# Three seven-product pairs in eight instead of two, and two pairs whose low parts are summed by DMA

## The chip, the cores and the metric

The kernel runs on one core of a Trainium2 chip. The metric is device time in microseconds (us) of one execution. Three runs of the kernel before took 2014.81, 2015.30 and 2015.38 us (median 2015.3). Engines: PE (TensorE, matmuls), PEld (its weight loads), DVE (VectorE), ACT (ScalarE), POOL (GpSimd), SP (SyncE, which here only issues DMAs).

## The reference

A decoder trunk of two layers on 256 tokens of width 2048, in float32. Each layer has attention (layer 0 a sliding window, layer 1 a block form that for 256 tokens is plain causal attention), attention to 256 memory tokens, and a feed-forward part of width 8192:

```
D_MODEL, SEQ, DEPTH, D_FF = 2048, 256, 2, 8192
mix = concat([self_out, mem_out]) @ w_o[layer]
h = layer_norm(ALPHA * h + mix, ln_g[layer, 0], ln_b[layer, 0])
ffn = jnp.square(jax.nn.relu(h @ w_up[layer])) @ w_down[layer]
h = layer_norm(ALPHA * h + ffn, ln_g[layer, 1], ln_b[layer, 1])
```

The change touches only the line with `ffn`.

## The kernel before

Each float32 operand is split into a high part, rounded to the matmul's type (`hi`, cast by ACT, line 97), and a low part, the rest (`lo`, subtracted by DVE, line 98). A product of two operands takes three matmuls: high x high, high x low, low x high (`mm3`, lines 269 to 273). The stationary side is a 128x128 tile of activations, the moving side 512 columns of weights.

The feed-forward part runs in four chunks of 2048 hidden columns per layer. A chunk has two up groups (`v_` = 0 and 1, 1024 hidden columns each) and two down groups (1024 output columns each). A group, `mlp_group`, covers 256 tokens x 1024 columns x 2048 of depth as eight pairs of 128-deep tiles; each pair's weights are one tile `raw` of 1 MB, loaded by SP. Twenty-nine groups run this way, 15 up and 14 down; the other three take another form (`aform`).

A plain pair has eight products, 24 matmuls. A fast pair has seven products by Strassen's scheme, 21 matmuls: `fast_weights` forms four differences of the weights in a tile `t` (DVE, lines 117, 120, 121) and splits seven blocks; `fast_acts` forms four sums of the activations (`x_f`, then `sums`). Four of the products, P1, P5, P6 and P7, go to PSUM banks of their own, which take turns with the banks of the transposes `pt_h`; `early` combines them. `UP` and `DOWN` (lines 69, 70) give the order of the pairs and how many are fast: pairs 0 and 1 of (2, 3, 0, 4, 1, 5, 6, 7).

At an up group's end DVE adds the banks and ACT applies relu and square; the result `u_n` is transposed to `gT` by PE in the next group, at the places that `UHOOKS` (line 71) names as (position of the pair, bank). In the second up group of a chunk `fast_acts(gt)` forms the sums for the down groups (hooks (5, 0) and (6, 0)). The first up group of layer 0 forms its sums from `hT` by hooks (0, 0) and (1, 1).

All engines run their queues in order. The order in which the queues stand is set by a scheduler at build time, and so is which of a pool's buffers a tile gets. What a pair may run ahead is limited by the pools: four buffers shared by `raw`, `t` and `x_f` (`NRAW`), seven for `whi`, seven for `wlo` (`NHI`).

Of the kernel before, what the change touches and what calls it, by code (L numbers as in the profile page):

```python
# [8 lines left out]
F32 = mybir.dt.float32  # L9
F32R = mybir.dt.float32r  # L10
I32 = mybir.dt.int32
AF = mybir.ActivationFunctionType
ALU = mybir.AluOpType
AX = mybir.AxisListType

P = 128
# [17 lines left out]
NRAW = 4  # L34
# [31 lines left out]
NWARM = 2  # L66
FILL = (10, 11, 12, 16)

UP = ((2, 3, 0, 4, 1, 5, 6, 7), 2)
DOWN = ((2, 3, 0, 4, 1, 5, 6, 7), 2)  # L70
UHOOKS = ((0, 3), (1, 0), (1, 2), (1, 3))
WTAIL = ((1, 2), (2, 0), (3, 1), (5, 2), (7, 1), (9, 2))


# [1 line left out]
def trunk(ctx: ExitStack, tc: tile.TileContext, a: dict, out: bass.AP):  # L76
# [19 lines left out]
    def split(hi, lo, src):  # L96
        nc.scalar.copy(hi, src)  # L97
        nc.vector.tensor_tensor(lo, src, hi.bitcast(F32), ALU.subtract)  # L98
# [26 lines left out]
    def fast_acts(xs, units):  # L125

        parts = []
        for j in range(0, len(units), 2):  # L130
            n = len(units[j:j + 2])
            x = xs[j // 2][:, :2 * n]
            raw = wp.tile([P, 2, 8, P], F32, name="x_f", tag="raw", bufs=NRAW)
            f = raw[:, 0, :4 * n].rearrange("p (k t) c -> p k (t c)", t=2)
            nc.vector.tensor_tensor(f, x[:, :, 0].bitcast(F32), x[:, :, 1].bitcast(F32), ALU.add)
            a11, a21 = f[:, 0:2 * n:2, :P], f[:, 0:2 * n:2, P:]
            a12, a22 = f[:, 1:2 * n:2, :P], f[:, 1:2 * n:2, P:]
            s = raw[:, 1, :4 * n].rearrange("p (u q) c -> p u q c", q=4)
            nc.vector.scalar_tensor_tensor(s[:, :, 0], a21, -1.0, a22, op0=ALU.mult, op1=ALU.subtract)
            nc.vector.scalar_tensor_tensor(s[:, :, 1], s[:, :, 0], -1.0, a11, op0=ALU.mult, op1=ALU.subtract)  # L140
            nc.vector.tensor_tensor(s[:, :, 2], a11, a21, ALU.subtract)
            nc.vector.tensor_tensor(s[:, :, 3], a12, s[:, :, 1], ALU.subtract)
            parts += [s[:, u] for u in range(n)]
        yield
        for (hi, lo), s in zip(units, parts):
            split(hi, lo, s)
        yield

    def sum_units(n, tags):
        units = []  # L150
        for tag in tags[:n]:
            if tag == "pts":
                units.append([ap_.tile([P, 4, P], F32R, name="sums", tag="pts", bufs=2) for _ in range(2)])
            else:
# [100 lines left out]
    def mlp_group(src, xts, sums, hooks, early, order, nfast):  # L255

        ps = [ps_mm.tile([P, 512], F32, name="ps_g", tag="mm") for _ in range(4)]
        own = {}  # L260
        seen = {}
        last = {}

        fast = ("P1", 0, 1, "P5", "P7", "P6", 2)
        for u in order:
            for i in range(7 if u < nfast else 4):
                last[fast[i] if u < nfast else i] = (u, i)

        def mm3(bank, x, w, st, en):
            (xh, xl), (hi, lo) = x, w  # L270
            nc.tensor.matmul(bank, xh, hi, start=st, stop=False)  # L271
            nc.tensor.matmul(bank, xh, lo, start=False, stop=False)  # L272
            nc.tensor.matmul(bank, xl, hi, start=False, stop=en)  # L273

        def tok(k, t):
            return [xts[k // 4][:, k % 4, s, t * P:(t + 1) * P] for s in range(2)]

        left = nfast
        for pos, u in enumerate(order):
            k0, k1 = 2 * u, 2 * u + 1  # L280
            if u < nfast:
                for i in range(4):
                    hooks.get((pos, i), nothing)()
                if not own:
                    for nm in ("P1", "P5", "P6", "P7"):
                        own[nm] = ps_at.tile([P, 512], F32, name=nm, tag="at")
                w = fast_weights(src[u])
                sx = [[s[:, q] for s in sums[u]] for q in range(4)]
                prods = (("P1", tok(k0, 0), "B11"), (0, tok(k1, 0), "B21"), (1, sx[3], "B22"),
                         ("P5", sx[0], "T1"), ("P7", sx[2], "T3"), ("P6", sx[1], "T2"), (2, tok(k1, 1), "T4"))  # L290
                for i, (b, x, wn) in enumerate(prods):
                    mm3(own[b] if b in own else ps[b], x, w[wn], b not in seen, last[b] == (u, i))
                    seen[b] = True
                left -= 1
                if not left:
                    early(own)
                continue
            (h0, l0), (h1, l1) = weights(src[u])
            w = {"B11": (h0[:, :512], l0[:, :512]), "B22": (h0[:, 512:], l0[:, 512:]),
                 "B12": (h1[:, :512], l1[:, :512]), "B21": (h1[:, 512:], l1[:, 512:])}  # L300
            for b in range(4):
                hooks.get((pos, b), nothing)()
                t, n = b // 2, b % 2 + 1
                mm3(ps[b], tok(k0, t), w[f"B1{n}"], b not in seen, False)
                mm3(ps[b], tok(k1, t), w[f"B2{n}"], False, last[b] == (u, b))
                seen[b] = True
        return ps


# [287 lines left out]
    for l in range(LAYERS):  # L597
# [34 lines left out]
        for c in range(FF // CH):  # L632
            gt = new_acts("og", "gT")
            todo = []
            sum_g = sum_units(DOWN[1], ("v", "mk"))
            for v_ in range(CH // 1024):

                hooks = dict(zip(UHOOKS, todo))
                us = [None] * 4
                if c == 0 and v_ == 0 and not more:  # L640
                    for nb in range(2):
                        ps, fin = aform([a["wup_s"][nb, i] for i in range(4)], hT, hold=(16 if nb == 0 else 0))
                        if nb == 0:
                            us[0] = relu2(ps[0])
                            fin()
                            us[2] = relu2(ps[1])
                        else:
                            us[1], us[3] = relu2(ps[0]), relu2(ps[1])
                else:
                    if sum_h is None:  # L650
                        sum_h = sum_units(UP[1], ("sum_h0", "sum_h1", "pts"))
                        steps = fast_acts(hT, sum_h)
                        hooks[0, 0] = hooks[1, 1] = lambda s=steps: next(s)
                    if v_ == 1:
                        steps = fast_acts(gt, sum_g)
                        hooks[5, 0] = hooks[6, 0] = lambda s=steps: next(s)
                    acc = []
                    ps = mlp_group(a["wup"][l, c * (CH // 1024) + v_], hT, sum_h, hooks, sums_up(acc), *UP)
                    for b in range(4):
                        nc.vector.tensor_tensor(acc[b], acc[b], ps[b], ALU.add)  # L660
                        nc.scalar.activation(acc[b], acc[b], AF.Relu)
                        nc.scalar.activation(acc[b], acc[b], AF.Square)
                    us = acc

                def back(b, v_=v_, us=us, gt=gt):
                    transposed(us[b], gt[2 * v_ + b % 2], b // 2, 0)
                todo = [lambda b=b, f=back: f(b) for b in (0, 1, 2, 3)]
            last = c == FF // CH - 1
            if last and more:
                memt = load_acts(a["memt"], "hT", "memt")  # L670
            for v_ in range(D // 1024):
                if last and v_ == 1:
                    for nb in range(2, 4):
                        ps, fin = aform([a["wdn_s"][l, nb - 2, i] for i in range(4)], gt,
                                        hold=(0 if nb == 2 else 8 if more else HOLDF))
                        if nb == 2:
                            for t in range(NT):
                                residual(h, ps, t, nb, False, st)
                    continue
# [68 lines left out]
```

## Time and profile before

| | us |
|---|---|
| median of three runs | 2015.3 |
| the profiled execution's own time | 2016.56 |
| its span | 2014.4 |
| PE busy | 1994.2 (99%) |
| DVE busy | 1543.9 (77%) |
| ACT busy | 1046.0 (52%) |
| POOL busy | 1.2 |
| chain that ended last | PE 96%, DVE 3% |

What an engine is busy with is summed over the span; what bounds the kernel is read from the chain that ended last and from stretches. Instructions on one engine overlap a little: the duration of one is longer than the step from one start to the next, and it is the step that counts when many follow each other. PE's matmuls are pipelined in the same way.

### The profile page before, as it was taken

The page shows a single profiled execution, that of the slowest core. Times are in us where ns is not written, and L with a number is a line of the kernel's source. Part 1 is how long each engine was busy: PE and PEld are TensorE (multiplying, and loading weights), DVE is VectorE, ACT ScalarE, POOL GpSimd, SP SyncE. Part 2 cuts the span into 40 slices and gives each one's busy share as a digit, 9 for nine tenths or more (in the row PEclk, how much of TensorE's full clock was granted, in tenths as well). Part 3 has the DMA queues.
Part 4 walks back from the last instruction along what each step waited for, and adds up shares of the span by engine and source line. Part 5 has one row for each costly group of instructions (what it writes and reads, how often), then busy time and mean ns, then how long its engine had stood idle before and what let it go on. Part 6 is the DMA issues. An engine that isn't in the chain of part 4 may idle for free.

```text
span 2014.4 us, 23998 instructions
## 1 busy us (share of the span) xinstructions
PE 1994.2 (99%) x9326; PEld 1662.3 (83%) x9326; DVE 1543.9 (77%) x1961; ACT 1046.0 (52%) x1361; POOL 1.2 (0%) x8
## 2 busy tenths in 40 slices
PE   9999999999999999999999999999999999999997
PEld 7888888888888888888888888778888888888886
DVE  6566659988787888878785665688878887878885
ACT  6455534654564555466444554346455545654651
POOL 0000000000000000000000000000000000000000
PEclk9999999999999999999999999999999999999999
DMA  9644554555456555456654446445564555555651
GB/s 336 251 160 152 191 185 169 215 203 207 169 186 225 214 177 194 172 188 240 245 225 168 160 160 204 147 146 188 206 216 184 190 186 188 199 218 191 238 209 73
DMA packets 56273, 391.63 MB, mean 194 GB/s; under 512 B 6368, under 2 KB 6368, under 8 KB 9696
## 3 DMA queue, kind: packets, MB, share of 16 engines
q1 hardware_dynamic: 56160, 390.10, 53.7%
q8 instruction: 73, 1.20, 0.2%
q14 instruction: 40, 0.33, 0.0%
HBM read 387.98 MB, written 2.10 MB: 194 GB/s over the span
## 4 chain that ended last, share of the span: by engine, by line
PE 96%; DVE 3%; issue 0%; DMA 0%; ACT 0%; SPq 0%; DVEq 0%
PE ps_g L271 18%; PE ps_g L273 18%; PE ps_g L272 18%; PE ps_w L209 7%; PE ps_a L231 5%; PE ps_a L232 5%; PE ps_a L233 5%; PE ps_w L211 4%; PE P L271 3%; PE P L273 3%; PE P L272 3%; PE pt_h L443 2%; PE ps_m L553 1%; PE ps_m L554 1%; PE ps_m L555 1%; DVE h L436 1%
## 5 line engine op out<-in xcount | busy, mean ns | idle before, releaser
L98 DVE TENSOR_TENSOR wlo<-raw,whi 128x1024 fp32r<-128x1024 f32 (+1 forms) x706 | 818.1, 1174 | 329.7 <-ACT whi L97 325.2
L97 ACT CAST whi<-raw 128x1024 fp32r<-128x1024 f32 (+1 forms) x706 | 697.2, 1014 | 624.5 <-PE ps_g L273 349.7
L271 PE MATMUL ps_g<-whi,hT 128*128 128x512 f32 x780 | 306.7, 393 | 0.0
L273 PE MATMUL ps_g<-whi,hT 128*128 128x512 f32 x780 | 303.8, 390 | 0.0
L272 PE MATMUL ps_g<-wlo,hT 128*128 128x512 f32 x780 | 303.7, 389 | 0.0
L271 PE MATMUL ps_g<-whi,gT 128*128 128x512 f32 x728 | 286.4, 393 | 0.0
L273 PE MATMUL ps_g<-whi,gT 128*128 128x512 f32 x728 | 283.7, 390 | 0.0
L272 PE MATMUL ps_g<-wlo,gT 128*128 128x512 f32 x728 | 283.4, 389 | 0.0
L273 PEld LDWEIGHTS ps_g<-whi,hT 128*128 128x128 f32 x780 | 146.4, 188 | 30.8
L271 PEld LDWEIGHTS ps_g<-whi,hT 128*128 128x128 f32 x780 | 146.5, 188 | 29.4
L272 PEld LDWEIGHTS ps_g<-wlo,hT 128*128 128x128 f32 x780 | 146.6, 188 | 29.3
L273 PEld LDWEIGHTS ps_g<-whi,gT 128*128 128x128 f32 x728 | 136.7, 188 | 28.9
L97 ACT CAST whi<-t 128x1024 fp32r<-128x1024 f32 x116 | 122.0, 1052 | 72.5 <-PE ps_g L273 45.1
L272 PEld LDWEIGHTS ps_g<-wlo,gT 128*128 128x128 f32 x728 | 136.8, 188 | 27.3
L271 PEld LDWEIGHTS ps_g<-whi,gT 128*128 128x128 f32 x728 | 136.7, 188 | 27.2
L98 DVE TENSOR_TENSOR wlo<-t,whi 128x1024 fp32r<-128x1024 f32 x116 | 141.5, 1222 | 20.9 <-ACT whi L97 20.5
L209 PE MATMUL ps_w<-hT,whi 128*128 128x512 f32 x320 | 119.9, 414 | 0.0
L209 PE MATMUL ps_w<-xT,whi 128*128 128x512 f32 x320 | 119.9, 414 | 0.0
L231 PE MATMUL ps_a<-whi,ot 128*128 128x512 f32 x256 | 101.7, 397 | 0.0
L233 PE MATMUL ps_a<-whi,ot 128*128 128x512 f32 x256 | 99.8, 390 | 0.0
L232 PE MATMUL ps_a<-wlo,ot 128*128 128x512 f32 x256 | 99.7, 389 | 0.0
L211 PE MATMUL ps_w<-xT,wlo 128*128 128x256 f32 x320 | 89.9, 281 | 0.0
(170 smaller groups left out, 2832.0 us busy)
## 6 DMA issues: line engine op xcount, KB each, us to landing
raw<-in_wup_dram SPq DMA_DIRECT2D x120, 1024.0 KB, 4.8
raw<-in_wdn_dram SPq DMA_DIRECT2D x112, 1024.0 KB, 4.9
raw<-in_wo_dram SPq DMA_DIRECT2D x32, 1024.0 KB, 4.8
raw<-in_wq_dram SPq DMA_DIRECT2D x24, 1024.0 KB, 4.8
raw<-in_wdn_s_dram SPq DMA_DIRECT2D x16, 1024.0 KB, 4.8
raw<-in_wmk_dram SPq DMA_DIRECT2D x8, 1024.0 KB, 6.2
raw<-in_wv_dram SPq DMA_DIRECT2D x8, 1024.0 KB, 7.3
raw<-in_wk_dram SPq DMA_DIRECT2D x8, 1024.0 KB, 4.9
```

Of the source, the lines that this page charges most:

```text
L97: nc.scalar.copy(hi, src)
L98: nc.vector.tensor_tensor(lo, src, hi.bitcast(F32), ALU.subtract)
L209: nc.tensor.matmul(ps, hi[:, kk:kk + P], x.rearrange("p s t -> p (s t)"), start=(k == 0), stop=False)
L211: nc.tensor.matmul(ps[:, :T], lo[:, kk:kk + P], x[:, 0], start=False, stop=(k == KT - 1))
L231: nc.tensor.matmul(ps[t], xh, hi, start=st, stop=False)
L232: nc.tensor.matmul(ps[t], xh, lo, start=False, stop=False)
L233: nc.tensor.matmul(ps[t], xl, hi, start=False, stop=en)
L271: nc.tensor.matmul(bank, xh, hi, start=st, stop=False)
L272: nc.tensor.matmul(bank, xh, lo, start=False, stop=False)
L273: nc.tensor.matmul(bank, xl, hi, start=False, stop=en)
L436: nc.vector.scalar_tensor_tensor(ht[:, c], ht[:, c], mean, g, op0=ALU.subtract, op1=ALU.mult)
L443: nc.tensor.transpose(pt[:, k], src[:, k * P:(k + 1) * P], ident)
```

## The change

The order becomes (3, 0, 4, 1, 5, 2, 6, 7) with three fast pairs, 0, 1 and 2. Pairs 3 and 6, first and seventh in the order, get their low parts in another way: ACT writes the negated high part into a buffer `dlo` (two pieces of 1024 columns), and a DMA issued by POOL adds the weights to it from DRAM. The matmuls with that low part, eight for a pair, are taken out of the pair (`mm2` issues the other sixteen) and issued later: those of pair 3 after the second pair, those of pair 6 at the end of its own. There is one buffer `dlo` for all. The transposes move to the first pair of a group and the start of the second. The sums of three pairs take two tiles `x_f` of the shared buffers instead of one; the third pair's are held in a new tag (`qt`) or in `pts`, and sums are split in pieces of 256. In layer 0 all steps of `fast_acts(hT)` are issued ahead of the first group.

```diff
-UP = ((2, 3, 0, 4, 1, 5, 6, 7), 2)
-DOWN = ((2, 3, 0, 4, 1, 5, 6, 7), 2)
-UHOOKS = ((0, 3), (1, 0), (1, 2), (1, 3))
+UP = ((3, 0, 4, 1, 5, 2, 6, 7), 3)
+DOWN = ((3, 0, 4, 1, 5, 2, 6, 7), 3)
+SUMMED = {3: 1, 6: 6}
+UHOOKS = ((0, 1), (0, 2), (0, 3), (1, 0))
...
         for (hi, lo), s in zip(units, parts):
-            split(hi, lo, s)
+            for q in range(2):
+                split(hi[q], lo[q], s[:, 2 * q:2 * q + 2])
...
+    def summed_weights(src):
+        raw = wp.tile([P, 2048], F32, name="raw", tag="raw", bufs=NRAW)
+        nc.sync.dma_start(raw, src)
+        lo = wp.tile([P, 2048], F32R, name="dlo", tag="dlo", bufs=1)
+        for c in (0, 1024):
+            nc.scalar.activation(lo[:, c:c + 1024], raw[:, c:c + 1024], AF.Copy, scale=-1.0)
+            nc.gpsimd.dma_start(lo[:, c:c + 1024], src[:, c:c + 1024], accum_op=ALU.add)
+        halves = []
+        for c in (0, 1024):
+            hi = wp.tile([P, 1024], F32R, name="whi", tag="whi", bufs=NHI)
+            nc.scalar.copy(hi, raw[:, c:c + 1024])
+            halves.append((hi, lo[:, c:c + 1024]))
+        return halves
...
+        def mm2(bank, x, w, st):
+            nc.tensor.matmul(bank, x[0], w[0], start=st, stop=False)
+            nc.tensor.matmul(bank, x[1], w[0], start=False, stop=False)
+        late = {}
+        def lates(pos):
+            for bank, x, lo in late.pop(pos, ()):
+                nc.tensor.matmul(bank, x, lo, start=False, stop=False)
...
-            (h0, l0), (h1, l1) = weights(src[u])
+            (h0, l0), (h1, l1) = (summed_weights if u in SUMMED else weights)(src[u])
...
-                mm3(ps[b], tok(k0, t), w[f"B1{n}"], b not in seen, False)
-                mm3(ps[b], tok(k1, t), w[f"B2{n}"], False, last[b] == (u, b))
-                seen[b] = True
+                if u in SUMMED:
+                    for k, nm in ((k0, f"B1{n}"), (k1, f"B2{n}")):
+                        mm2(ps[b], tok(k, t), w[nm], b not in seen)
+                        seen[b] = True
+                        late.setdefault(SUMMED[u], []).append((ps[b], tok(k, t)[0], w[nm][1]))
+                else:
...
+            lates(pos)
...
-            sum_g = sum_units(DOWN[1], ("v", "mk"))
+            sum_g = sum_units(DOWN[1], ("v", "mk", "pts"))
...
-                        hooks[0, 0] = hooks[1, 1] = lambda s=steps: next(s)
+                        if more:
+                            list(steps)
+                        else:
+                            hooks[0, 0] = lambda s=steps: next(s)
+                            hooks[0, 2] = lambda s=steps, f=hooks[0, 2]: (f(), next(s))
```

Three places show what that does to the queues. In the rows a name's number tells tiles apart; `raw_4852` is one load, `t` and `x_f` are as above.

The first is DVE's queue in the second up group of layer 0's second chunk, where the sums of `gT` are formed, from the end of one fast pair on. Before:

```order
L98 TENSOR_TENSOR wlo_4718<-t_4707,whi_4717 128x1024
L135 TENSOR_TENSOR x_f_4767<-gT0_4199 128x1024
L98 TENSOR_TENSOR wlo_4724<-t_4707,whi_4723 128x1024
L98 TENSOR_TENSOR wlo_4760<-raw_4757,whi_4759 128x1024
L139 SCALAR_TENSOR_TENSOR x_f_4767<-x_f_4767 128x2x128
L141 TENSOR_TENSOR x_f_4767<-x_f_4767 128x2x128
L140 SCALAR_TENSOR_TENSOR x_f_4767<-x_f_4767 128x2x128
L142 TENSOR_TENSOR x_f_4767<-x_f_4767 128x2x128
L98 TENSOR_TENSOR sums_4203<-x_f_4767,sums_4203 128x512
L98 TENSOR_TENSOR wlo_4764<-raw_4757,whi_4763 128x1024
L98 TENSOR_TENSOR wlo_4800<-raw_4797,whi_4799 128x1024
```

And now, from the last low part of the fifth pair (`raw_4806`) on:

```order
L100 TENSOR_TENSOR wlo_4813<-raw_4806,whi_4812 128x1024
L100 TENSOR_TENSOR sums_4281<-x_f_4840,sums_4281 128x256 x2
L119 TENSOR_TENSOR t_4854<-raw_4852 128x1024
L100 TENSOR_TENSOR wlo_4856<-raw_4852,whi_4855 128x1024
L100 TENSOR_TENSOR wlo_4861<-raw_4852,whi_4860 128x512
L100 TENSOR_TENSOR wlo_4865<-t_4854,whi_4864 128x1024
L122 TENSOR_TENSOR t_4854<-raw_4852,t_4854 128x512
L100 TENSOR_TENSOR sums_4282<-x_f_4840,sums_4282 128x256
L123 TENSOR_TENSOR t_4854<-raw_4852,t_4854 128x512
L100 TENSOR_TENSOR sums_4282<-x_f_4840,sums_4282 128x256
L100 TENSOR_TENSOR sums_4284<-x_f_4846,sums_4283 128x256 x2
L100 TENSOR_TENSOR wlo_4871<-t_4854,whi_4870 128x1024
```

Behind the work on the sums there stood the plain pairs; now the third fast pair (`raw_4852`, sixth in the order) stands there, with its differences and four low parts, and the sums are worked on in between. The load of the seventh pair (`raw_4904`) gets the buffer of `raw_4852` and waits for its last reader, the row of line 123.

The second is ACT's queue at the same place. Before:

```order
L97 CAST whi_4759<-raw_4757 128x1024
L97 CAST sums_4203<-x_f_4767 128x512
L97 CAST whi_4763<-raw_4757 128x1024
L97 CAST whi_4799<-raw_4797 128x1024
L503 COPY u_n_4748<-P1_4624 128x512
L97 CAST whi_4803<-raw_4797 128x1024
L97 CAST sums_4204<-x_f_4767 128x512
L97 CAST whi_4837<-raw_4835 128x1024
L97 CAST whi_4841<-raw_4835 128x1024
```

And now:

```order
L99 CAST whi_4812<-raw_4806 128x1024
L99 CAST sums_4281<-x_f_4840 128x256 x2
L99 CAST sums_4282<-x_f_4840 128x256 x2
L99 CAST sums_4283<-x_f_4846 128x256 x2
L99 CAST whi_4855<-raw_4852 128x1024
L99 CAST whi_4860<-raw_4852 128x512
L99 CAST whi_4864<-t_4854 128x1024
L99 CAST whi_4870<-t_4854 128x1024
L545 COPY u_n_4895<-P1_4674 128x512
L174 ACTIVATE dlo_4906<-raw_4904 128x1024 x2
L179 CAST whi_4911<-raw_4904 128x1024
L179 CAST whi_4913<-raw_4904 128x1024
```

The seventh pair takes four instructions of ACT instead of two, and the two that write `dlo` stand ahead of the two casts that PE needs first.

The third is ACT's queue where layer 0's feed-forward part begins: `mv` copies the last result of the memory projection, `hT3` are the last transposed activations. Before:

```order
L97 CAST whi_2867<-raw_2861 128x1024
L445 CAST hT1_2759<-pt_h_2760 128x4x128
L445 CAST hT1_2759<-pt_h_2767 128x4x128
L445 CAST hT2_2780<-pt_h_2781 128x4x128
L445 CAST hT2_2780<-pt_h_2788 128x4x128
L313 COPY mv_2844<-ps_m_2646 128x512
L313 COPY mv_2844<-ps_m_2647 128x512
L445 CAST hT3_2829<-pt_h_2830 128x4x128
L445 CAST hT3_2829<-pt_h_2837 128x4x128
L97 CAST sums_2855<-x_f_2871 128x512
L97 CAST sums_2856<-x_f_2871 128x512
L97 CAST whi_2903<-raw_2901 128x1024
```

And now:

```order
L355 COPY mv_2844<-ps_m_2646 128x512
L355 COPY mv_2844<-ps_m_2647 128x512
L487 CAST hT3_2829<-pt_h_2830 128x4x128
L487 CAST hT3_2829<-pt_h_2837 128x4x128
L99 CAST sums_2860<-x_f_2869 128x256
L174 ACTIVATE dlo_2893<-raw_2891 128x1024 x2
L179 CAST whi_2898<-raw_2891 128x1024
L179 CAST whi_2900<-raw_2891 128x1024
L99 CAST whi_2925<-raw_2922 128x1024
```

The casts of the group's first pair stood ahead of the copies of `mv` (`raw_2861`; `raw_2901` is the second pair); now those of the first pair (`raw_2891`) stand behind the copies, the last transposes and two instructions for `dlo`.

## Rows read from the trace of the kernel before

**Rows 1.** The page: span, busy time of each engine, chain that ended last
```profile
span 2014.4 us, 23998 instructions
PE 1994.2 (99%) x9326; PEld 1662.3 (83%) x9326; DVE 1543.9 (77%) x1961; ACT 1046.0 (52%) x1361; POOL 1.2 (0%) x8
...
PE 96%; DVE 3%; issue 0%; DMA 0%; ACT 0%; SPq 0%; DVEq 0%
```

**Rows 2.** Busy time by stretch: us, each engine busy (instructions), clock, DMA share, GB/s
```profile
345.00:1010.00 665.00, 665.00 (x2996) 550.66 (x2995) 550.96 (x616) 366.36 (x430) 0.00 (x0) 1.00 0.56 204
```

**Rows 3.** Timeline of PE in an up group: start, duration, line, instruction
```profile
700.01 0.39 PE L272 MATMUL P<-wlo,sums 128*128 128x512 f32 x1
...
711.79 0.39 PE L273 MATMUL ps_g<-whi,hT 128*128 128x512 f32 x1
```

**Rows 4.** DMA view: queue's share; issues, count, KB each, median us to landing
```profile
q1 hardware_dynamic: 56160, 390.10, 53.7%
...
raw<-in_wup_dram SPq DMA_DIRECT2D x120, 1024.0 KB, 4.8
raw<-in_wdn_dram SPq DMA_DIRECT2D x112, 1024.0 KB, 4.9
...
raw<-in_wv_dram SPq DMA_DIRECT2D x8, 1024.0 KB, 7.3
...
out_dram<-h SPq DMA_DIRECT2D x8, 256.0 KB, 2.5
...
ln_row<-in_ln_g_dram SPq DMA_DIRECT2D x2, 512.0 KB, 3.8
```

**Rows 5.** Timeline of DVE in a second up group, where the sums are formed
```profile
717.66 0.69 DVE L660 TENSOR_TENSOR u_n<-u_n,ps_g 128x512 f32<-128x512 f32 x1 [0.67 <-PE ps_g L273]
...
733.74 1.22 DVE L98 TENSOR_TENSOR wlo<-t,whi 128x1024 fp32r<-128x1024 f32 x1
734.88 1.22 DVE L135 TENSOR_TENSOR x_f<-gT 128x1024 f32<-128x1024 f32 x1
...
737.14 1.22 DVE L98 TENSOR_TENSOR wlo<-raw,whi 128x1024 fp32r<-128x1024 f32 x1
738.28 0.42 DVE L139 SCALAR_TENSOR_TENSOR x_f<-x_f 128x256 f32<-128x256 f32 x1
738.62 0.42 DVE L141 TENSOR_TENSOR x_f<-x_f 128x256 f32<-128x256 f32 x1
...
745.59 0.69 DVE L98 TENSOR_TENSOR sums<-x_f,sums 128x512 fp32r<-128x512 f32 x1
746.19 0.68 DVE L505 TENSOR_TENSOR u_n<-u_n,P 128x512 f32<-128x512 f32 x1
```

**Rows 6.** Timeline of SP's queue in the same group
```profile
746.30 0.33 SPq L105 DMA_DIRECT2D raw<-in_wdn_dram  x1
```

**Rows 7.** Timeline of ACT in the same group
```profile
742.76 1.05 ACT L97 CAST whi<-raw 128x1024 fp32r<-128x1024 f32 x1
743.72 0.62 ACT L97 CAST sums<-x_f 128x512 fp32r<-128x512 f32 x1
744.24 2.00 ACT L97 CAST whi<-raw 128x1024 fp32r<-128x1024 f32 x2
747.56 1.05 ACT L97 CAST whi<-raw 128x1024 fp32r<-128x1024 f32 x1 [1.33 <-DMA raw<-in_wdn_dram]
```

**Rows 8.** Chain that ended last, where layer 0's first group begins: start, us
```profile
329.64 0.87 PE pt_h L443 x8
330.52 0.23 PE ps_g L271
```

**Rows 9.** Timeline of ACT at the same place
```profile
320.83 1.05 ACT L97 CAST whi<-raw 128x1024 fp32r<-128x1024 f32 x1
...
329.00 1.27 ACT L313 COPY mv<-ps_m 128x512 f32<-128x512 f32 x2 [4.14 <-PE ps_m L555]
330.16 1.08 ACT L445 CAST hT<-pt_h 128x512 fp32r<-128x512 f32 x2
331.12 1.16 ACT L97 CAST sums<-x_f 128x512 fp32r<-128x512 f32 x2
```

More of the change, by code (lines that the diff above doesn't have):

```diff
@@ L152, in sum_units @@
             if tag == "pts":
-                units.append([ap_.tile([P, 4, P], F32R, name="sums", tag="pts", bufs=2) for _ in range(2)])
+                t_ = [ap_.tile([P, 4, P], F32R, name="sums", tag="pts", bufs=2) for _ in range(2)]
+                units.append([[t[:, :2], t[:, 2:]] for t in t_])
+            elif tag == "qt":
+                t_ = [ap_.tile([P, 2, P], F32R, name="sums", tag="qt", bufs=4) for _ in range(4)]
+                units.append([t_[:2], t_[2:]])
             else:
                 t_ = ap_.tile([P, 2, 4, P], F32R, name="sums", tag=tag)
-                units.append([t_[:, s] for s in range(2)])
+                units.append([[t_[:, s, :2], t_[:, s, 2:]] for s in range(2)])
         return units
+    def summed_weights(src):
[11 more added lines that the diff above has]
+        return halves
     def weights(src, parts=1):
@@ L287, in mlp_group @@
                 w = fast_weights(src[u])
-                sx = [[s[:, q] for s in sums[u]] for q in range(4)]
+                sx = [[s[q // 2][:, q % 2] for s in sums[u]] for q in range(4)]
                 prods = (("P1", tok(k0, 0), "B11"), (0, tok(k1, 0), "B21"), (1, sx[3], "B22"),
@@ L303, in mlp_group @@
                 t, n = b // 2, b % 2 + 1
-                mm3(ps[b], tok(k0, t), w[f"B1{n}"], b not in seen, False)
-                mm3(ps[b], tok(k1, t), w[f"B2{n}"], False, last[b] == (u, b))
-                seen[b] = True
+                if u in SUMMED:
[4 more added lines that the diff above has]
+                else:
+                    mm3(ps[b], tok(k0, t), w[f"B1{n}"], b not in seen, False)
+                    mm3(ps[b], tok(k1, t), w[f"B2{n}"], False, last[b] == (u, b))
+                    seen[b] = True
+            lates(pos)
         return ps
@@ L650, in trunk @@
                     if sum_h is None:
-                        sum_h = sum_units(UP[1], ("sum_h0", "sum_h1", "pts"))
+                        sum_h = sum_units(UP[1], ("sum_h0", "sum_h1", "qt"))
                         steps = fast_acts(hT, sum_h)
-                        hooks[0, 0] = hooks[1, 1] = lambda s=steps: next(s)
+                        if more:
[3 more added lines that the diff above has]
+                            hooks[0, 2] = lambda s=steps, f=hooks[0, 2]: (f(), next(s))
                     if v_ == 1:
@@ L739 @@
     }
-    nc = bacc.Bacc("TRN2", target_bir_lowering=False, num_devices=1, dynamic_dma_scratch_size=1024)
+    nc = bacc.Bacc("TRN2", target_bir_lowering=False, num_devices=1, dynamic_dma_scratch_size=2048)
     args = {k: nc.dram_tensor(f"in_{k}_dram", v.shape, mybir.dt.from_np(v.dtype), kind="ExternalInput").ap()
```

## The prediction

> **What bounds the kernel now.** I read the page first: of a span of 2014.4 us PE is busy 99%, DVE 77%, ACT 52%, and PE is 96% of the chain that ended last [rows 1]. The view by stretch then shows that there is no slack on PE in the feed-forward part of layer 0: 665.00 of 665.00 us, while DVE works 551 and ACT 366 [rows 2]. So the time there is the number of matmuls times the step from one to the next, and every gap that opens on PE is lost for good. The step comes from the timeline of PE: the first and the last of 53 matmuls start 11.78 us apart, 52 steps of 0.2265 us [rows 3] (the duration of 0.39 is the pipeline's and not what one costs). DVE and ACT run beside PE and matter only where a part comes too late.
>
> **What goes.** A third fast pair saves three matmuls a group, 21 for 24. The loads count the groups: (120 + 112) / 8 = 29 [rows 4]. 29 x 3 x 0.2265 = 19.7 us, all of it on the path. The summed pairs keep their 24 matmuls, eight of them later.
>
> **What comes, on DVE and ACT, over a whole group.** Steps: DVE 1.14 us for 1024 columns, 0.60 for 512, 0.34 for 256 [rows 5]; ACT 0.96 for 1024, 0.52 for 512 [rows 7]. A plain pair is 2 x 1.14 on DVE; a fast one 4 x 1.14 + 3 x 0.60 = 6.4; a summed one nothing. Before 2 x 6.4 + 6 x 2.3 = 26.4 us a group, now 3 x 6.4 + 3 x 2.3 = 26.0, of 183 x 0.2265 = 41.4 us of PE. ACT goes from 18.2 to 23.6 (four writes of 1024 for a summed pair). Neither becomes the bound on the whole, so I charge nothing here; the covers are those 41.4 us. What can cost is a place where the parts come too late, because the three fast pairs (second, fourth, sixth) press DVE together: 3 x 6.4 + 2 x 2.3 = 23.8 of its 26.0 us come before the seventh pair. I find two such places.
>
> **First place: the second up group of each chunk.** There DVE also forms the sums of gT. I add up its queue from the group's start to line 123 of the sixth pair, the row after which the buffer of that pair's weights is free and the seventh pair's load is issued: thirteen instructions of 1024 columns (last low part of the second pair, differences and three low parts of the fourth, the third and fifth pairs, one of x_f, difference and two low parts of the sixth), twelve of 512, seven of 256, four of 128 for which I take 0.2 each (no such row; between nothing and 0.34): 14.8 + 7.2 + 2.4 + 0.8 = 25.2 us. The queue starts about 0.3 us after the group's start, with the last of four adds, which waits for PE [rows 5], and waits some 0.5 for the copies of gT: line 123 ends at 26.0. An issue follows within 0.1 us of the reader's end (745.59 + 0.69 on DVE, 746.30 on SP [rows 5, 6]); a load of 1 MB lands in 4.8 [rows 4], so at 30.9. That a late load stops ACT happens before too: at 747.56 it had waited 1.33 us for one [rows 7], with nothing behind it. Now four steps of ACT follow, the two halves of dlo and the two casts: 31.0 + 3 x 0.96 + 1.05 = 34.9 for the second cast. PE reaches the seventh pair after 135 matmuls and 16 transposes of 0.109 (0.87 for eight [rows 8]): 30.6 + 1.7 = 32.3 us. Its third matmul needs the second cast, at 32.8. PE waits 34.9 - 32.8 = 2.1 us. Before, this wait did not arise: x_f took one of the four buffers and plain pairs came behind it.
>
> The same pair's low part: the second half of dlo is written at 33.0, and PE, after its wait, comes to the late matmuls 14 steps on, at 38.1, so the DMA may take 5.1 us. No row shows an adding DMA or any DMA from POOL. Nearest rows: 256 KB in 2.5 us, 512 KB in 3.8, and at the slow end 1 MB in 7.3 [rows 4]. The engines' share, 53.7% of 2014.4 us for 390.1 MB, is 2.8 us per MB, so a load of 4.8 is 2.0 plus its bytes. If the addition costs no more than a load, the halves are there at 35.4 and 36.4: no wait. If each half counts twice (DRAM and the buffer are both read), the second queues behind the first and is there at 32.0 + 2.0 + 5.6 = 39.6: a wait of 1.5 us. By the ends 2.5 and 7.3 it is 0 to 2.2. I take 0.7, the middle of the two cases.
>
> The Trainium skill (Collectives: The Full Stack, "The bandwidth ceiling: the fold count and why AG ≠ RS ≠ AR") says that an addition inside the DMA engines is slow not by its arithmetic but "because the add needs **two source reads**". No run here shows it; by it the wait would be 1.5 us in each such group and the forecast below 6 us higher, and by a single read 5 us lower.
>
> Behind the wait ACT's queue is late into the next group: the casts of the eighth pair, the next first pair, its dlo (released only by the late matmuls) and the relus follow, and the fourth copy of gT leaves DVE about 8.6 us into that group. P7, which takes the bank of the fourth transposes, is due at 16 + 21 steps less the last nine, and the transposes: 28 x 0.2265 + 1.7 = 8.1. 0.5 us.
>
> Together 2.1 + 0.7 + 0.5 = 3.3 us. Of eight such groups the order lets one escape: in layer 1's first chunk the seventh load gets the buffer of the fifth pair, free some 6 us sooner. 7 x 3.3 = 23.1 us.
>
> **Second place: the start of layer 0's feed-forward part.** Before, the first pair's casts were made at 320.83 [rows 9], and PE went from the last transposes (329.64 + 0.87) straight to its first product at 330.52 [rows 8]. Now they stand behind the copies of mv and hT3, which end at 331.24 [rows 9], a cast of the sums and two writes of dlo. From 331.15: 0.3 + 3 x 0.96 + 1.05 gives 335.4 for the second cast, which PE wants at 330.52 + 0.45: 4.4 us, once. In layer 1 the first group follows other feed-forward matmuls and ACT stands some pairs ahead of PE: nothing.
>
> **Elsewhere** I charge nothing. In the other 22 groups the seventh pair's load gets a buffer free about 10 us earlier. The first pair's dlo waits for the late matmuls of the group before; then PE has 24 + 16 + 21 steps, 13.8 us, less 2.2 for ACT: the DMA may take 11.6 us. Behind that waiting ACT instruction stand casts of the fast pair, which PE needs 5 us later than the wait ends. The transposes come after the squares: the fourth square ends 2.8 us into the group, its transposes are at 4.9. POOL has nothing else to do. The added reads raise the load on the DMA engines from 8 MB a group to between 10 and 12, 28 to 33 us of 41.4; that can lengthen landings, and every us at the seventh pair costs 7.
>
> **Sum.** Against the profiled execution's own 2016.56 (span 2014.4 and 2.2 around it): - 19.7 + 23.1 + 4.4 = + 7.8, 2024.4; the median of the runs shown is 1.3 below that execution, so 2023. By the ends (0.8 to 7.8 us in each of the seven groups: the small instructions free and no wait for gT, or a landing of 7.3) 2006 to 2055.
>
> **Rivals.** *The gain stands.* Line 123 of the sixth pair ends 2 us earlier than I add up, the seventh load is in time, the sums take no longer than a load: 2015.3 - 19.7 + 4.4 = 2000, faster. It decides from line 123 at 23.9 us after the group's start. For it: DVE's step has no overlap with its waits in my sum, and I took every instruction of the queue in series. Against it: nothing in those 26 us is idle but 0.8.
>
> *The sum is slow.* The DMA on POOL takes 10 us instead of about 6. Then the seven groups wait 4 us more, 28 us: 2051; from 11.6 us on the first pairs of all groups wait too, 29 us in all for each us more. For it: two reads, a queue shared with 1 MB loads, slowest row 7.3. Against: 512 KB in 3.8.
>
> **Chances.** Forecast 0.52 (its own range 2011 to 2036), gain stands 0.27 (1996 to 2011), slow sum 0.21 (2036 and up). Within 0.2%, 4 us, a measurement of this kernel cannot tell a change from none. Faster: 0.24 of the second case and 0.01 of the first, 0.25. Same: 0.12 of the first, 0.03 and 0.02 of the others, 0.17. Slower: 0.39 and 0.19, 0.58. The range runs from 1999 to 2050: it leaves out a tenth above and less below.
>
> **What would show it.** Right: 87 matmuls fewer; waits of PE for casts of line 179 in seven second up groups, 2 us each, with ACT waiting for the seventh load just before; one wait of about 4.4 us at the start of layer 0's first group; line 123 of the sixth pair about 26 us into the group. Wrong: PE without gaps in those groups (then 2000), or waits of the late matmuls in every group (then the DMA decides).

## The result

The changed kernel takes 2233.7 us (median of four runs, 2230.9 to 2239.3); the kernel before, on the same chip, 2015.1. The ratio is 1.109, 95% interval 1.107 to 1.111: 218 us slower, where 8 were forecast. The page after (span, busy time, chain by engine), for [rows 1]:

```profile
span 2237.6 us, 24398 instructions
PE 2049.8 (92%) x9239; PEld 1675.3 (75%) x9239; DVE 1544.5 (69%) x2080; ACT 1195.8 (53%) x1575; POOL 102.0 (5%) x124
...
PE 37%; DMA 32%; DVE 23%; ACT 4%; issue 3%; POOL 0%; SPq 0%; ACTq 0%; DVEq 0%; POOLq 0%
```

The 87 matmuls are gone (9326 to 9239). PE's idle time is 2237.6 - 2049.8 = 187.8 us, against 2014.4 - 1994.2 = 20.2 before: 167.6 more. PE's busy time went up by 55.6 instead of down by 19.7: the same matmuls take 75 us more. Some 55 of these are a lower clock (granted on average 0.964 over the span, before 0.997; weighed over PE's busy time alone, what the clock lacked of its full rate is 56.9 us, before 1.7). Of the other 20 some 13 can be put down, by estimate, to the ends of idle stretches: the trace has 87 of them on PE where there were 5, and at each the last matmul counts with its 0.39 us and not with the step of 0.23. Idle and busy time together give 167.6 + 55.6 = 223.2, the difference of the spans. The chain, once 96% PE, is a third DMA. The DMA view, for [rows 4] (queue: packets, MB, share of the engines; then issues, KB each, median us to landing):

```profile
q1 hardware_dynamic: 56160, 390.10, 47.8%
q0 software_dynamic: 16704, 60.82, 15.3%
...
raw<-in_wup_dram SPq DMA_DIRECT2D x120, 1024.0 KB, 6.7
raw<-in_wdn_dram SPq DMA_DIRECT2D x112, 1024.0 KB, 6.4
...
dlo<-in_wup_dram POOLq DMA_DIRECT2D x60, 512.0 KB, 10.3
dlo<-in_wdn_dram POOLq DMA_DIRECT2D x56, 512.0 KB, 10.6
```

A half of `dlo` lands after 10.3 to 10.6 us by the median of all halves; taken apart, the first half of a pair lands after 9.3 and the second, issued behind it, after 12.4. The loads beside it need 6.4 to 6.7 in place of 4.8 to 4.9. In time on the engines the sum costs 0.153 x 2237.6 / 60.82 = 5.6 us per MB, a load 2.7. Who waits, PE first, then DVE (us in all, times, longest):

```profile
PE ps_g L307 <- DMA dlo<-in_wup_dram: 74.0, 25, 5.4
PE ps_g L307 <- DMA dlo<-in_wdn_dram: 42.5, 16, 4.3
PE ps_g L300 <- ACT whi L179: 19.1, 9, 3.9
PE P L295 <- DVE gT L488: 14.2, 11, 2.2
PE ps_g L300 <- DVE u_n L706: 12.0, 6, 2.3
```

```profile
DVE t L119 <- DMA raw<-in_wup_dram: 97.2, 25, 8.0
DVE t L119 <- DMA raw<-in_wdn_dram: 80.4, 31, 5.6
```

The late matmuls (line 307) wait 116.5 us for the sum. Read pair by pair, 112.4 of these are at the seventh pair, in every one of the 29 groups: 58.6 in the seven second up groups that the prediction charged and 53.8 in the other 22. The first pairs wait 4.1 us in all. DVE waits 177.6 us for loads of fast pairs; before, it waited 1.2:

```profile
DVE t L117 <- DMA raw<-in_wdn_dram: 0.9, 3, 0.4
DVE t L117 <- DMA raw<-in_wup_dram: 0.3, 1, 0.3
```

How a late load reaches PE is seen at one seam, the start of a second up group; by stretch (us, each engine's busy time and instructions, clock, DMA share, GB/s):

```profile
761.00:773.00 12.00, 12.00 (x55) 9.93 (x54) 2.42 (x3) 6.71 (x8) 0.86 (x1) 1.00 1.02 290
...
783.00:785.00 2.00, 0.00 (x0) 0.00 (x0) 2.00 (x4) 0.00 (x0) 0.00 (x0) 0.96 0.99 152
785.00:787.00 2.00, 1.83 (x4) 1.38 (x5) 1.82 (x4) 1.88 (x4) 0.00 (x0) 0.50 0.94 176
787.00:789.00 2.00, 2.00 (x10) 1.72 (x9) 0.49 (x1) 2.00 (x4) 0.00 (x0) 0.68 1.07 301
```

Two halves were issued at 759.79 and 761.82 and three loads between 758.22 and 762.23; the share of the DMA engines is 1.02 for 12 us (a packet is counted where it starts, so a stretch can come out over 1). The last of these loads takes 13.35 us in the chain (first fence); DVE stands 7.99 us at line 119 for it, and in its queue behind that stand the adds of the group's results (`u_n`, second fence), which PE needs for its banks:

```profile
762.23 13.35 DMA raw<-in_wup_dram
775.57 0.02 issue
775.60 1.23 DVE t L119
```

```profile
775.60 1.23 DVE L119 TENSOR_TENSOR t<-raw 128x1024 f32<-128x1024 f32 x1 [7.99 <-DMA raw<-in_wup_dram]
...
784.34 2.48 DVE L706 TENSOR_TENSOR u_n<-u_n,ps_g 128x512 f32<-128x512 f32 x4
```

PE does nothing from 783 to 785, and after that idle its granted clock is 0.50 and 0.68 for four microseconds, the lower of its two levels (1.2 GHz) and a mix of both with the upper (2.4 GHz). That is how one idle stretch costs twice.

### The profile page after: what moved, and what is told of

The parts are those of the page before. It is cut to its first block, busy times and chain, and to the rows that moved or that the text cites. A ratio compares the mean times of both kernels' runs of the same rounds, so it can differ in the third digit from the quotient of the medians.

```text
span 2237.6 us, 24398 instructions
## 1 busy us (share of the span) xinstructions
PE 2049.8 (92%) x9239; PEld 1675.3 (75%) x9239; DVE 1544.5 (69%) x2080; ACT 1195.8 (53%) x1575; POOL 102.0 (5%) x124
## 3 DMA queue, kind: packets, MB, share of 16 engines
q0 software_dynamic: 16704, 60.82, 15.3%
## 4 chain that ended last, share of the span: by engine, by line
PE 37%; DMA 32%; DVE 23%; ACT 4%; issue 3%; POOL 0%; SPq 0%; ACTq 0%; DVEq 0%; POOLq 0%
DVE wlo L100 12%; DMA raw<-in_wup_dram 10%; DMA raw<-in_wdn_dram 8%; DMA dlo<-in_wdn_dram 7%; PE ps_w L233 7%; DMA dlo<-in_wup_dram 5%; PE ps_a L255 5%; PE ps_a L257 5%; PE ps_a L256 5%; PE ps_w L235 3%; PE ps_g L307 3%; DVE t L119 3%; ACT dlo L174 2%; ACT whi L99 1%; DVE t L123 1%
## 5 line engine op out<-in xcount | busy, mean ns | idle before, releaser
L100 DVE TENSOR_TENSOR wlo<-raw,whi 128x1024 fp32r<-128x1024 f32 (+1 forms) x590 | 658.9, 1139 | 277.7 <-ACT whi L99 275.7
L99 ACT CAST whi<-raw 128x1024 fp32r<-128x1024 f32 (+1 forms) x590 | 567.1, 984 | 407.7 <-PE ps_a L257 149.2
L100 DVE TENSOR_TENSOR wlo<-t,whi 128x1024 fp32r<-128x1024 f32 x174 | 211.6, 1222 | 47.3 <-ACT whi L99 47.2
L119 DVE TENSOR_TENSOR t<-raw 128x1024 f32<-128x1024 f32 x87 | 106.5, 1224 | 177.7 <-DMA raw<-in_wup_dram 97.2
L174 ACT ACTIVATE dlo<-raw 128x1024 fp32r<-128x1024 f32 x116 | 118.2, 1053 | 141.9 <-PE ps_g L307 99.2
L295 PE MATMUL ps_g<-whi,hT 128*128 128x512 f32 x450 | 178.5, 397 | 0.0
L296 PE MATMUL ps_g<-wlo,hT 128*128 128x512 f32 x450 | 177.4, 394 | 0.0
L297 PE MATMUL ps_g<-whi,hT 128*128 128x512 f32 x450 | 176.7, 393 | 0.0
L295 PE MATMUL ps_g<-whi,gT 128*128 128x512 f32 x420 | 167.2, 398 | 0.0
L296 PE MATMUL ps_g<-wlo,gT 128*128 128x512 f32 x420 | 166.3, 396 | 0.0
L297 PE MATMUL ps_g<-whi,gT 128*128 128x512 f32 x420 | 165.9, 395 | 0.0
L179 ACT CAST whi<-raw 128x1024 fp32r<-128x1024 f32 x116 | 117.5, 1045 | 50.3 <-PE ps_g L297 24.7
L300 PE MATMUL ps_g<-whi,hT 128*128 128x512 f32 x240 | 103.5, 431 | 29.6 <-ACT whi L179 16.9
L295 PE MATMUL P<-whi,sums 128*128 128x512 f32 x261 | 103.0, 395 | 1.5 <-DVE gT L488 1.5
## 6 DMA issues: line engine op xcount, KB each, us to landing
dlo<-in_wup_dram POOLq DMA_DIRECT2D x60, 512.0 KB, 10.3
dlo<-in_wdn_dram POOLq DMA_DIRECT2D x56, 512.0 KB, 10.6
```

What stands on the lines that cost most here:

```text
L119: nc.vector.tensor_tensor(t_[:, 0:2], b[:, 0:2], b[:, 2:3].broadcast_to([P, 2, 512]), ALU.subtract)
L174: nc.scalar.activation(lo[:, c:c + 1024], raw[:, c:c + 1024], AF.Copy, scale=-1.0)
L179: nc.scalar.copy(hi, raw[:, c:c + 1024])
```

## The experiments

Theory 1: the adding DMA is the loss, by its own length and by what it does to the loads. Theory 2: three fast pairs and the new order are, by the four shared buffers and DVE's queue. Theory 3: the software queue of POOL is slow, whether it adds or not. "The crowd" below stands for what transfers in flight at the same time cost each other. Each row is the median of four runs (the first of ten), against the kernel before on the same chip.

| kernel | median us | ratio to before, interval |
|---|---|---|
| no sum | 2016.3 | 1.001 (1.000 to 1.002) |
| plain copies in place of sums | 2102.7 | 1.044 (1.042 to 1.045) |
| late matmuls read another tile | 2213.1 | 1.098 (1.097 to 1.100) |
| sums that nobody waits for | 2136.6 | 1.061 (1.059 to 1.062) |
| three fast pairs, no summed ones | 2033.4 | 1.009 (1.007 to 1.010) |
| two fast pairs, two summed | 2141.9 | 1.063 (1.062 to 1.065) |
| before, with sums at the front | 2100.0 | 1.042 (1.041 to 1.044) |
| before, with tied sums | 2081.2 | 1.033 (1.031 to 1.035) |
| seventh pair alone summed | 2193.1 | 1.088 (1.086 to 1.090) |
| first pair alone summed | 2048.8 | 1.017 (1.015 to 1.019) |
| second sum in the fifth place | 2087.4 | 1.035 (1.034 to 1.037) |
| low parts on POOL | 2124.5 | 1.054 (1.052 to 1.056) |
| three fast pairs where DVE has room | 2005.9 | 0.995 (0.994 to 0.997) |

**Without the sum.** The DMA is left out; ACT's writes stay.

```diff
-            nc.gpsimd.dma_start(lo[:, c:c + 1024], src[:, c:c + 1024], accum_op=ALU.add)
```

> The changed kernel without its adding DMAs; the low parts of the two summed pairs stay the negated high parts, so the sum is left out of the computation. Theory 1 (the adding DMA and what it does to the other transfers is the loss): 2015 to 2030 us, TensorE idle in the span back to 20 to 40 us, the wide loads landing in 4.8 to 5.2 us (median) again. Theory 2 (three fast pairs and the new order are the loss, by the load ring and VectorE's queue): stays above 2150 us.

2016.3 us: theory 2 falls. Its page row and PE's largest wait:

```profile
PE 1981.3 (98%) x9239; PEld 1647.7 (82%) x9239; DVE 1544.3 (77%) x2080; ACT 1194.1 (59%) x1575; POOL 1.2 (0%) x8
```

```profile
PE ps_g L299 <- ACT whi L178: 12.3, 9, 3.9
```

With the DMA away, the matmuls saved are just paid back: of the span 2014.6, 33.3 us are idle (13.1 more than before), and busy is 1981.3 where 1994.2 - 19.7 = 1974.5 was due, 6.8 us of clock. That POOL's issuing slows DVE is ruled out too: DVE's low parts of 128x1024 take 1222 ns on average in the changed kernel and 1219 here. The trace also shows how long a sum may take: from the second write of `dlo` to the first late matmul. First ACT, then PE, in the end of one group and the start of the next:

```profile
749.90 2.01 ACT L174 ACTIVATE dlo<-raw 128x1024 fp32r<-128x1024 f32 x2 [1.25 <-DMA raw<-in_wup_dram]
758.78 2.01 ACT L174 ACTIVATE dlo<-raw 128x1024 fp32r<-128x1024 f32 x2 [1.18 <-PE ps_g L306]
```

```profile
756.70 0.62 PE L306 MATMUL ps_g<-dlo,hT 128*128 128x512 f32 x2
774.22 1.07 PE L306 MATMUL ps_g<-dlo,gT 128*128 128x512 f32 x4
```

The seventh pair of this second up group: 756.70 - 751.91 = 4.8 us. The first pair behind it: 13.4. Read so for every group, the seventh pair has 4.8 us in seven second up groups and 8.6 to 12.4 in the others; the first pair has 11.6 to 13.5 in nearly all. The second half needs 12.4 in the changed kernel: the seventh pairs of the seven groups miss by far, those of the others by less (they wait 0.4 to 5.1 us there), and the first pairs lie at the edge.

**Plain copies.** The subtraction of the high part is left out.

```diff
-  nc.gpsimd.dma_start(lo[...], src[...], accum_op=ALU.add)
+  nc.gpsimd.dma_start(lo[...], src[...])
```

> The changed kernel with its 116 adding DMAs made plain copies of the same size, queue and place; the low parts of the summed pairs are then copies of the weights, so the subtraction of the high part is left out. Theory 1, narrow form (the second read is what costs): 2020 to 2060 us, landing near 5 us, 2.7 us of the 16 DMA engines per MB. Theory 3 (GpSimd's software queue is slow, whether it adds or not): above 2150 us, landing near 10 us.

2102.7: between the two. Copying the weights a second time costs 86 us over the run without it, the addition 131 more. Theory 1's narrow form was too cheap by 43 us: a copy too is crowded, landing in 7.4 to 7.5 us, the loads in 5.0 to 6.0.

**The price with nothing beside it.** Five DMAs of 512 KB into a buffer that nobody reads, one behind the other, at the end of the kernel before.

```diff
...
+ nc.gpsimd.dma_start(x, y, accum_op=ALU.add)
+ nc.gpsimd.dma_start(x, y)
+ nc.sync.dma_start(x, y)
+ nc.gpsimd.dma_start(x, y, accum_op=ALU.add)
+ nc.gpsimd.dma_start(x, y)
```

> The kernel before, with five DMAs of 512 KB behind each other at its end, where no load is under way: adding (GpSimd), plain (GpSimd), plain (SyncE), adding, plain. If the doubling of bytes alone makes the adding DMA slow: plain 3.5 to 4.5 us, adding 5 to 6 us, and the 10.6 us in the changed kernel are the crowd. If the addition is slow by itself: adding 8 us or more with nothing beside it.

It was run once (2017.6 us). Timelines, POOL first, then SP (start, duration, line; in brackets the idle time before and what ended it):

```profile
1984.63 1.01 POOL L684 DMA_DIRECT2D extra<-in_wdn_s_dram  x1 [0.32 <-POOL extra L683]
1991.48 0.56 POOL L685 DMA_DIRECT2D extra<-in_wdn_s_dram  x1 [5.84 <-DMA extra<-in_wdn_s_dram]
1999.51 0.86 POOL L687 DMA_DIRECT2D extra<-in_wdn_s_dram  x1 [7.48 <-DMA extra<-in_wdn_s_dram]
```

```profile
1995.51 0.33 SPq L686 DMA_DIRECT2D extra<-in_wdn_s_dram  x1
```

From issue to the next issue: adding 1991.48 - 1984.63 = 6.85 us, plain on POOL 1995.51 - 1991.48 = 4.03, plain on SP 1999.51 - 1995.51 = 4.00. From issue to landing they are 6.6, 4.0 and 3.7. So theory 3 falls as a matter of the queue; the addition makes 2.6 to 2.8 us, and the crowd, the pair's other half with it, turns 6.6 into 10.3 to 10.6. The time alone lies between the two expectations (below 6 and above 8). The second addition, with the output's stores beside it, took 7.55. The Trainium skill (Collectives: The Full Stack, "The bandwidth ceiling: the fold count and why AG ≠ RS ≠ AR") puts the price of an addition in a reduction between cores down to two source reads. The engines' time per MB agrees: 5.6 us in the changed kernel against 0.092 x 2100.1 / 60.82 = 3.2 for the plain copies, 1.8 times. The second read itself is in no row.

**Who waits.** The late matmuls read another tile (that part of the product is left out).

```diff
-  nc.tensor.matmul(bank, x, lo, start=False, stop=False)
+  nc.tensor.matmul(bank, x, xts[0][:, 0]..., start=False, stop=False)
```

> The changed kernel with all its adding DMAs, but the late matmuls of the summed pairs read another tile that has long been there, so TensorE doesn't wait for the sum (that part of the product is left out). If the direct waits of TensorE for the sum are the loss: 118 of the 168 us of new idle and their share of the clock go, near 2080 us. If the crowded transfers are most of it (late loads, VectorE's queue behind them): above 2140 us.

2213.1, 21 us less. PE's wait moved rather than went: there is one `dlo`, and now ACT waits for the DMA before it may write the next (134.6 us in all, up to 11.3 at a time), with the casts for DVE and PE behind it in its queue. PE now waits for DVE's adds, 71.9 us at the largest row where it was 12.0:

```profile
ACT dlo L174 <- DMA dlo<-in_wup_dram: 88.6, 9, 11.3
```

```profile
PE ps_g L300 <- DVE u_n L706: 71.9, 20, 7.4
```

So the sums were next given a buffer that neither reads, ACT's writes put into the high part's tile, and the DMAs tied to their places by a copy of four columns on POOL:

```diff
+  nc.scalar.activation(hi, raw[:, c:c + 1024], AF.Copy, scale=-1.0)
+  nc.gpsimd.tensor_copy(extra[:, c:c + 4], hi[:, :4].bitcast(F32))
+  nc.gpsimd.dma_start(extra[:, c:c + 1024], src[:, c:c + 1024], accum_op=ALU.add)
```

> The changed kernel with 116 adding DMAs of the same size at the same places, but into a buffer that nobody reads, each tied by a copy of four columns of that pair's high part on GpSimd; ScalarE's negated writes go into the high part's tile ahead of the cast, and the late matmuls of the summed pairs read another tile (that part of the product is left out). Neither TensorE nor ScalarE waits for a sum. Crowding alone makes the loss: 2130 to 2220 us, wide loads above 6 us. The waits for the sum itself (TensorE's, and ScalarE's for the one buffer of it) make it: 2020 to 2080 us.

2136.6: sums that nobody waits for cost 120 of the 217 us over the run without them, at the low end of what was expected; the other 97 go with the waits. DVE waits 153.8 us for loads at the fast pairs' first difference here too. The places are not quite the same: the small copies wait for the sum before, since all share one buffer (131.0 us in 43 of 116), so sums come later and further apart.

**The sums without the third fast pair.** Order and hooks of before, `SUMMED = {2: 2, 6: 6}`; then the kernel before with sums into an unused buffer, first free to run, then tied as above.

```diff
+  nc.gpsimd.tensor_copy(extra[:, c:c + 4], h[:, :4].bitcast(F32))
+  nc.gpsimd.dma_start(extra[:, c:c + 1024], src[u][:, c:c + 1024], accum_op=ALU.add)
```

> The order, hooks and two fast pairs of the kernel before, with the third and the seventh unit summed by the adding DMA and used late. Theory 1: the sums are the loss with the order of before too, 2100 to 2200 us, wide loads above 6 us (median). Theory 2 (it takes three fast pairs): 2010 to 2040 us.

> The kernel before, with two adding DMAs of 512 KB put in at the third and the seventh pair's place of each group, into a buffer that nobody reads. If the crowding reaches the loads of any order: 2040 to 2120 us, wide loads landing in 6 to 7 us. If it hurts only where three fast pairs leave the loads no slack: 2015 to 2025 us.

> The kernel before with two adding DMAs of 512 KB at the third and the seventh pair of each group into a buffer that nobody reads, each tied to its place by a copy of four columns of that pair's high part on GpSimd (in the run before without that tie they all ran in the first quarter). If crowding alone costs wherever it falls: 2060 to 2130 us. If the loads of the kernel before have slack to give: 2015 to 2030 us though wide loads land in 6 us or more.

2141.9, 2100.0 and 2081.2. The second ran all its sums at the front, where nothing held them (DMA busy 90% and more in the first 11 of 40 slices), so its 85 us say only that crowding hurts the order of before too. In the third the loads land in 6.5 to 6.7 us, DVE waits 124.7 us for them, and the loss is 66 us: before had no slack to give. In the first PE hardly waits for a sum:

```profile
PE ps_g L300 <- DVE u_n L702: 33.8, 23, 4.0
PE P L295 <- DVE gT L488: 22.6, 30, 1.4
PE ps_g L300 <- DVE h L492: 14.3, 10, 2.6
...
PE ps_g L307 <- DMA dlo<-in_wdn_dram: 4.0, 5, 1.3
PE ps_g L307 <- DMA dlo<-in_wup_dram: 2.8, 6, 1.3
```

Its 127 us come mostly by way of DVE: PE's new idle time is 86.5 us, and the first three rows make 70.7 of it; DVE waits 182.2 us for loads, then come the adds behind them.

**Which place.** `SUMMED = {}`, then `{6: 6}` alone, then `{3: 1}` alone.

> Three fast pairs in the new order, all low parts by VectorE again, no adding DMA. Theory 1 (the adding DMA is the loss): VectorE gets 58 pairs x 2.28 us = 132 us more work than in the run without the sum (2016.3 us), so 2015 to 2045 us. Theory 2 (three fast pairs and the new order are the loss): above 2100 us.

> The changed kernel with only the seventh pair summed by DMA (58 adding DMAs instead of 116), the first pair's low parts on VectorE again. If the loss goes with the number of adding DMAs: half of the 218 us over the run without the sum, plus some 10 us for VectorE, 2110 to 2150 us. If it is the seventh pair's place that is bad: above 2170; the first pair's: below 2080.

> The changed kernel with only the first pair of each group summed by DMA (58 adding DMAs), the seventh pair's low parts on VectorE. With only the seventh pair summed 2193.1 us were measured, 177 above the run without the sum. If it is the seventh pair's short way to its use: 2030 to 2090 us, hardly a wait of TensorE for a sum. If any 58 adding DMAs cost that: 2150 to 2210 us.

2033.4, 2193.1 and 2048.8. The same 58 DMAs cost 160 us over the run with none at the seventh pair and 15 at the first. With the seventh alone DVE waits only 9.7 us for loads at line 119 (with the first alone 54.9): 103.6 us of waits for the sum and 40 us more of PE's busy time make most of the 160. Waits of PE for the sum, seventh alone, then first alone:

```profile
PE ps_g L307 <- DMA dlo<-in_wup_dram: 77.3, 24, 5.8
PE ps_g L307 <- DMA dlo<-in_wdn_dram: 26.3, 9, 4.2
```

```profile
PE ps_g L307 <- DMA dlo<-in_wdn_dram: 0.4, 1, 0.4
PE ps_g L307 <- DMA dlo<-in_wup_dram: 0.4, 1, 0.4
```

Then the changed kernel with units 5 and 6 exchanged, so that a fast and a plain pair stand between the second sum's pair and the end of the group:

```diff
-UP = ((3, 0, 4, 1, 5, 2, 6, 7), 3)
+UP = ((3, 0, 4, 1, 6, 2, 5, 7), 3)
```

(`DOWN` likewise; the late matmuls stay at the seventh place.)

> The changed kernel with unit 6 in the fifth place and unit 5 in the seventh, so that the second summed pair has the 21 matmuls of the last fast pair and the 24 of a plain pair, 10 us, before its late matmuls. If the waits for the sum at the seventh place make the part that crowding alone does not: 2120 to 2170 us, TensorE's waits for dlo under 30 us in place of 116. If the crowd and the loads behind it decide wherever the sum stands: above 2190 us.

2087.4: 146 us less than the changed kernel, better than expected. PE's waits for the sum fall from 116.5 to 2.8 us, though the loads land still later (7.7 to 8.3 us). What is left over the run without sums, 71 us, is then mostly the crowd. This is less than the 120 of the run in which nobody waits, whose sums stand at the seventh place and whose POOL makes 116 small copies. Two things differ, and neither was tried apart: the place of the sums, and DVE's work, since unit 6 now relieves DVE ahead of the last fast pair (no run has this order without sums). So the loss splits into waits and crowd as 97 and 120 us by one run and as 146 and 71 by the other; that both parts are there is shown, which is the larger is not.

**Other ways to the low parts.** POOL subtracts, with neither the negated write nor the DMA:

```diff
...
+  nc.gpsimd.tensor_tensor(lo[:, c:c + 1024], raw[:, c:c + 1024], hi.bitcast(F32), ALU.subtract)
```

> The changed kernel with the low parts of the summed pairs made by a subtraction on GpSimd instead of the negated write on ScalarE and the adding DMA. Theory 1: no DMA, so wide loads land in 4.8 us again; 2000 to 2030 us if GpSimd takes under 3 us for 128x1024 and doesn't slow VectorE, slower by what it does slow it. Theory 2: above 2100 us.

2124.5, slower by far, with loads at 4.8 us. Groups of instructions (busy us, mean ns, idle before): POOL's row of this run, DVE's of this run, and DVE's of the run without sums:

```profile
L177 POOL TENSOR_TENSOR dlo<-raw,whi 128x1024 fp32r<-128x1024 f32 x116 | 321.2, 2785 | 1730.6 <-ACT whi L176 1551.5 <-PE ps_g L305 143.1 <-PE ps_g L295 35.9
```

```profile
L100 DVE TENSOR_TENSOR wlo<-raw,whi 128x1024 fp32r<-128x1024 f32 (+1 forms) x590 | 734.9, 1267 | 264.1 <-ACT whi L99 261.6
```

```profile
L100 DVE TENSOR_TENSOR wlo<-raw,whi 128x1024 fp32r<-128x1024 f32 (+1 forms) x590 | 657.9, 1137 | 280.4 <-ACT whi L99 278.0
```

A subtraction takes POOL 2.8 us, and DVE's same instructions become 11% longer on average. The Trainium skill (SBUF — State Buffer, "Who interferes with whom") says that a DVE instruction with two SBUF inputs contends with a GpSimd instruction that reads SBUF; the rows agree. PE waits only 6.2 us for POOL's own low parts, and 53.9 for DVE's adds (`h`, `u_n`): here PE stops for a slower DVE though the loads are on time.

Last, three fast pairs only in the first up group of each chunk and in the down groups; the second up groups, where DVE also forms the sums, keep two. All low parts are DVE's, and the sums of `hT` in layer 0 have the hooks of before.

```diff
+UP2 = ((2, 3, 0, 4, 1, 5, 6, 7), 2)
+UHOOKS2 = ((0, 3), (1, 0), (1, 2), (1, 3))
+SUMMED = {}
-                hooks = dict(zip(UHOOKS, todo))
+                hooks = dict(zip(UHOOKS2 if v_ else UHOOKS, todo))
...
-  ps = mlp_group(..., sums_up(acc), *UP)
+  ps = mlp_group(..., sums_up(acc), *(UP2 if v_ else UP))
```

> No sums by DMA. Third fast pair only in the first up group of each chunk and in the down groups (7 and 14 of 29 groups); the second up group, where VectorE also forms the sums of gT, keeps two and the order of before. 21 x 3 x 0.2265 = 14.3 us fewer matmuls; with three fast pairs everywhere the waits were mostly in up groups. 2001 to 2012 us if they were in the second ones; 2015 to 2030 us if the third fast pair overloads VectorE anywhere.

2005.9 us, the fastest of all: 0.46% under the kernel before (0.30 to 0.63%). Its page:

```profile
span 2004.7 us, 24194 instructions
PE 1981.4 (99%) x9263; PEld 1649.1 (82%) x9263; DVE 1640.6 (82%) x2156; ACT 1084.8 (54%) x1443; POOL 1.2 (0%) x8
```

63 matmuls less are 14.3 us; busy fell by 12.8, and idle rose by 23.3 - 20.2 = 3.1.

## Why the prediction was wrong

The direction was right, the size wrong by 210 us. Step by step:

- *What goes*: right. 87 matmuls less.
- *First place and second place, without the sum*: right in place, too dear in size. In the run without the sum line 123 of the sixth pair ends 25.6 to 25.8 us into the seven groups (26.0 forecast), and PE waits there 0.7 to 1.2 us for the casts of the seventh pair, 6.2 together (seven times 2.1 forecast, 14.7). At layer 0's start it waits 3.9 us (4.4 forecast), for the copy of `gT` not at all (0.5 each forecast), and 2.2 us in a place that I had not seen, for the casts of a first pair, in the down group behind layer 0's last second up group. That the time of this run comes out at 2016.3, where these terms alone gave 2015.3 - 19.7 + 7 x 2.6 + 4.4 = 2018, is partly luck: the waits were 10 us too dear, and 6.8 us of clock, which I had not counted, made up most of that.
- *"so the DMA may take 5.1 us"* and, for the first pairs, *"the DMA may take 11.6 us"*: right, 4.8 and, in nearly all groups, 11.6 to 13.5 measured; the first pairs wait 4.1 us in the whole kernel. That the seventh pairs of the other 22 groups have only 8.6 to 12.4 us I did not look at.
- *"I take 0.7, the middle of the two cases"*: the first step that failed. I worked out a half from the loads' engine time, at 4.8 us for two reads and 6.6 for the second half behind the first. Alone one half takes 6.6 to land; in this kernel the second halves take 12.4. The seventh pair waits 6.9 to 9.7 us for its sum in the seven groups (58.6 together, 4.9 forecast), and 53.8 us in the other 22, where I put the wait at nothing.
- *"Elsewhere I charge nothing"*, with *"that can lengthen landings, and every us at the seventh pair costs 7"*: the second. I gave the crowd no price; alone it costs 71 to 120 us by the runs above. The loads went to 6.4 to 6.7 us, and with four shared buffers a late load stops DVE, in whose queue the adds and copies for PE stand. I counted the load on the engines by the average, 28 to 33 us of 41.4, where the stretch shows it at 1.02 for 12 us on end. The kernel before loses 66 us to the same number of sums without anyone waiting for them.
- *"every gap that opens on PE is lost for good"*, priced at its length: too cheap. Beside 168 us of new idle time some 55 us are matmuls at the lower clock.

Of the rivals, "gain stands" would have needed no waits in the second up groups. "The sum is slow" named the right cause with a price of 36 us where 218 were lost: it had the DMA's 10 us and the chance that first pairs wait, but left the loads at 4.8 us and the other 22 seventh pairs without a wait. The queue that it shares with the loads is not what the DMA view shows: the sums have their own (q0), and what they share is the engines.

## What to carry to other kernels

Where a change adds a kind of transfer that the trace does not show, price it twice: alone, and among the transfers that it meets in the same few microseconds; then hold the second price against the time to its use at every place it stands, not at the worst one only. Where loads arrive just in time, as they do in this ring of four buffers, a slower load can become a wait of the engine that works on it first, and of all that stands behind in that engine's queue. A costlier scheme that pays in some groups is best put into those alone: three fast pairs where DVE had room gained 9 us, and in all groups, with the low parts still DVE's, they lost 18.

## What the runs showed of the hardware

- An adding DMA of 512 KB from DRAM into SBUF took 6.85 us alone from its issue to the next one (6.6 to its landing), a plain one 4.0 on either queue. In time of the DMA engines the adding DMAs of the changed kernel cost 5.6 us per MB, the plain copies in their place 3.2; among the other transfers of the changed kernel an adding DMA landed in 5.5 to 15.3 us.
- With sums under way the DMA engines' share was 1.02 over 12 us that moved 290 GB/s, and 0.99 over 2 us that moved 152; plain loads of 1 MB took up to 13.35 us.
- POOL's 116 subtractions of 128x1024 (2.8 us each) came with DVE subtractions 11% longer.
- After 2.3 us without a matmul the granted clock was 0.50 over the next two and 0.68 over two more, although PE was busy again.
